# Twelve gate projections beside the long convolution, and the attention share of the mix in the stage behind it

## The chip, the core and the metric

The kernel runs on one core of a Trainium2 chip. The core has five engines that each work through their own queue strictly in order: PE (matrix multiplies), DVE (vector operations), ACT (activation functions and copies), POOL (elementwise, slower) and SP, which starts the DMA transfers here. Semaphores tie the queues together. The metric is the device time of one execution in microseconds (us); the time before is 1934.45 us, the median of three runs (1933.97 to 1934.61).

## What is computed

Two blocks of two layers each work on a sequence of 512 tokens of width 1024, in float32. The change touches the two layers of the first block. Of such a layer the reference says:

```python
q, k, v, z_a, u_h, z_h, g_a, g_h = jnp.split(rms_norm(x) @ w_in, ...)
o = diff_attention(q, k, v, ...)                       # 4 heads
y_a = rms_norm(o) * jax.nn.silu(z_a)                   # 512 x 512
hv, hx1, hx2 = jnp.split(short_conv3(u_h, ...), 3, axis=-1)
z = fft_long_conv(hv, filt[:, 0], ...) * hx1           # order 0
z = fft_long_conv(z, filt[:, 1], ...) * hx2            # order 1
y_h = z * jax.nn.silu(z_h)                             # 512 x 512
m = jax.nn.sigmoid(g_a) * (y_a @ w_pa) + jax.nn.sigmoid(g_h) * (y_h @ w_ph)
x = x + rms_norm(m @ w_out)
```

`g_a` and `g_h` are the gates: each is 1024 channels, eight groups of 128. They need only the normed input, so they may be computed at any time in the layer. `y_a @ w_pa` needs the attention; `y_h @ w_ph` needs the end of the convolution.

## The kernel before

Activations stand as 128 channels by 512 tokens. Each matrix product is made of three passes over a high and a low half of both operands (`mm3`, lines 261 to 263). A **projection** (`projT` over the 1024 input channels) is 24 matmuls of 512 columns into one bank of PSUM; a **branch** (`projT` over 512 channels) is 12. Either takes its weights from `wchunk`: a 512 KB transfer into one of two buffers `wr`, then ACT makes the high half `wh` (line 269) and DVE the low half `wl` (line 270), which for every third chunk is POOL's. PSUM banks for projections come in turn from two `acc` and one `fl`.

`gate` is one projection and a tanh on ACT. `branch` is 12 matmuls; its result is read by a DVE instruction that multiplies it with the gate plus one (line 854 for the attention's share, line 901 for the convolution's).

`hyena` is the long convolution. It runs over two orders `o` and two halves `g` of the channels, four **rounds** in all. One round is a chain through the engines:

- DVE makes sums and differences `sds`, `qd` of two channel groups (lines 751 to 755); PE transposes them (761); ACT and DVE split the result into `sd`.
- For `j` = 0, 1: PE multiplies with the transform into two `lg` banks, 12 matmuls of 256 columns (`px`, `py`); ACT copies one to `ys`; DVE rotates into `w` (784 to 788), multiplies with the filter's spectrum `hs` (791, 792); POOL adds (793, 794); DVE rotates into `Y[j]` (798 to 802).
- For each of the two channel groups: one projection with its short convolution into `hx` (in order 1 a second one, `gz`), the inverse transform as eight matmuls into the one `av` bank (820), which need `Y[0]` and `Y[1]`; DVE takes `e` out of the bank (822), makes `y` (824 to 828), and POOL multiplies `y` with `hx` into the next `z` (829).

Order 1 of a half starts from order 0's `z`. After every `j` step `hyena` calls `next(br)`, which runs one step of `branch_a`: one attention branch for f = 0 to 3, and a gate plus a branch for f = 4 to 7 (the gates 0 to 3 were made beside the attention). After `hyena` the mix stage splits `z` into `yh` and does, for eight `f`, a gate projection, a branch of `yh`, and the chain DVE (901), POOL (902), ACT (272), DVE (273) that leaves the output `m` in two halves. `out1` behind it multiplies with `w_out`.

The kernel is written in this order, but the order of each engine's queue is set at build time by a scheduler, which simulates the program with its own costs. It can pull independent projections forward and put them where it believes PE would wait.

Of the kernel before, what the change touches and what calls it, by code (L numbers as in the profile page):

```python
# [11 lines left out]
F32R = mybir.dt.float32r  # L12
# [4 lines left out]
ADD, SUB, MUL, MAX = ALU.add, ALU.subtract, ALU.mult, ALU.max  # L17

P = 128
S = 512  # L20
# [151 lines left out]
class Kern:  # L172
# [554 lines left out]

    def hyena(self, l, h, br):

        nc, A = self.nc, self.A  # L730
        fbh = self.sm(8, "fbh")
        nc.vector.tensor_scalar(fbh, self.c1[:, C1_FB:C1_FB + 8], 0.25, None, op0=MUL)
        z = self.z
# [3 lines left out]
        iv = self.T("iv", (P, 2, 2, P))  # L737
        nc.sync.dma_start(iv, A["inv"])
        stt = nc.vector.scalar_tensor_tensor
        halves = lambda t: t.rearrange("p (m two) -> p two m", two=2)  # L740
        for o in range(2):
            zn = self.U() if o == 0 else z
            for g in range(2):
                qd = []
                sd_hi = self.T("sd", (P, 2, 2, 256), F32R)
                sd_lo = self.T("sd", (P, 2, 2, 256), F32R)
                for c in range(2):
                    u = z[:, 2 * g + c]
                    up, down = halves(u[:, 0:256]), halves(u[:, 511:255:-1])
                    sd = self.T("sds", (P, 4, P))  # L750
# [14 lines left out]
                for j in range(2):  # L765
# [34 lines left out]
                    else:  # L800
                        stt(x, w[0], cot, w[1], op0=MUL, op1=ADD)
                        stt(y, w[1], cot, w[0], op0=MUL, op1=SUB)
                    next(br, None)
                for c in range(2):
# [23 lines left out]
                    nc.vector.tensor_tensor(halves(y[:, 511:255:-1]), ee[:, 0:2], ee[:, 2:4], op=SUB)  # L828
                    nc.gpsimd.tensor_tensor(zn[:, ct], y, hx, op=MUL)
            z = zn  # L830
        return z
# [12 lines left out]

    def branch_a(self, l, h, ya, ma):

        ma.append(self.U())
        for f in range(8):
            if f % 2 == 0:
                wch = self.wchunk(self.A[f"wpa{l}"][f // 2], 4, 256)  # L850
            t = ma[f // 4][:, f % 4]
            if f > 3:
                self.gate(l, h, 32 + f, t)
            self.nc.vector.scalar_tensor_tensor(t, t, 1.0, self.branch(ya, f, wch), op0=ADD, op1=MUL)
            yield

    def layer1(self, l, h):
# [20 lines left out]
        if "ya" in self.dbg:  # L878
            self.dump(ya, "ya")
        with self.stage(f"h{l}", dict(Y=4, iv=1, hx=2, gz=1, e=2, y=1)), \  # L880
                self.stage(f"i{l}", dict(sd=2, sds=2, qd=4, hs=4, w=4, ab=2)):
            br = self.branch_a(l, h, ya, ma)
            z = self.hyena(l, h, br)
            for _ in br:
                pass
        with self.stage(f"g{l}", dict(mm=4)):
            mh = [self.T("mm", (P, 4, S), F32R) for _ in range(2)]
            ml = [self.T("mm", (P, 4, S), F32R) for _ in range(2)]
            with self.stage(f"y{l}", dict(yh=2, m=3)):
                yh, yl = self.T("yh", (P, 4, S), F32R), self.T("yh", (P, 4, S), F32R)  # L890
                for c in range(4):
                    self.split(z[:, c], yh[:, c], yl[:, c], scale=0.5)
                yhp = [(yh[:, k], yl[:, k]) for k in range(4)]
                if "yh" in self.dbg:
                    self.dump(yhp, "yh")
                for f in range(8):
                    if f % 2 == 0:
                        wch = self.wchunk(A[f"wph{l}"][f // 2], 4, 256)
                    m = self.T("m")
                    self.gate(l, h, 40 + f, m)  # L900
                    nc.vector.scalar_tensor_tensor(m, m, 1.0, self.branch(yhp, f, wch), op0=ADD, op1=MUL)  # L901
                    nc.gpsimd.tensor_tensor(m, m, ma[f // 4][:, f % 4], op=ADD)  # L902
                    self.split(m, mh[f // 4][:, f % 4], ml[f // 4][:, f % 4], scale=0.5)
            m = [(mh[k // 4][:, k % 4], ml[k // 4][:, k % 4]) for k in range(8)]
            with self.stage(f"o{l}", dict(post=1, y1=2, sq2=1, gain=1, sq=1, xn=2)):
                self.out1(l, m)
# [709 lines left out]
```

## Time and profile before

| | us |
|---|---|
| median of three runs | 1934.45 |
| the profiled execution, its own time | 1933.28 |
| span of the profiled execution, first to last instruction | 1931.5 |
| long convolution of layer 0, with the end of the attention | about 200 to 370 |
| mix stage of layer 0 | about 370 to 440 |
| long convolution of layer 1, with the end of the attention | about 690 to 843 |
| mix stage of layer 1 | about 843 to 920 |

PE counts as busy for 97% of the span. A matmul of 512 columns is shown with some 0.39 us, but the next one starts 0.225 us later: they are pipelined, so the busy share hides small losses. What the engine loses shows as idle time between matmuls, and as stretches in which its granted clock is below 1.00.

### The profile page before, as it was taken

The numbers are of one execution on the slowest core, as the hardware profiler recorded it, in microseconds if no ns is written. First come the engines' busy times: TensorE is split into PE (matmuls) and PEld (weight loads), VectorE is DVE, ScalarE is ACT, GpSimd is POOL, SyncE is SP. The second block draws the span as 40 slices with busy tenths as digits, with TensorE's granted clock in tenths as the row PEclk, the third lists the DMA queues.
The fourth block names the chain that finished last, engine by engine and source line by source line (L and its number), as shares of the span: only waits on it lengthen the run. The fifth ranks groups of instructions, "written<-read, shape, count | busy, mean of one in ns | idle before, by whom it ended". The sixth has DMA issues, their size and how long they took to land.

```text
span 1931.5 us, 26186 instructions
## 1 busy us (share of the span) xinstructions
PE 1882.2 (97%) x9632; PEld 1565.8 (81%) x9632; DVE 1294.6 (67%) x2278; ACT 890.4 (46%) x1732; POOL 653.9 (34%) x555
## 2 busy tenths in 40 slices
PE   8999989999999899999999999999999999999998
PEld 5878878888788777888888877888889887788886
DVE  5888698634698868864558856667244886666722
ACT  4666412334476532233456355556324635556631
POOL 2445344432245524533135424211113532421111
PEclk9999989999999999999999999999999999999999
DMA  5333423224323333323432231212343223111232
GB/s 180 105 115 97 158 88 97 100 98 164 113 96 115 101 127 99 109 98 120 133 111 77 82 90 39 64 49 82 131 143 101 77 77 96 39 64 47 84 131 87
DMA packets 88392, 192.35 MB, mean 100 GB/s; under 512 B 28258, under 2 KB 38498, under 8 KB 88264
## 3 DMA queue, kind: packets, MB, share of 16 engines
q1 hardware_dynamic: 69592, 184.84, 29.2%
q10 hardware_dynamic: 17376, 3.67, 1.0%
q0 software_dynamic: 1296, 2.16, 0.4%
q8 instruction: 76, 1.25, 0.3%
q14 instruction: 52, 0.43, 0.1%
HBM read 172.28 MB, written 18.37 MB: 99 GB/s over the span
## 4 chain that ended last, share of the span: by engine, by line
PE 52%; DVE 6%; ACT 1%; issue 1%; POOL 1%; DMA 1%; ACTq 1%; POOLq 0%; DVEq 0%
PE acc L263 8%; PE acc L262 8%; PE acc L261 8%; PE fl L261 4%; PE fl L262 4%; PE fl L263 4%; PE av L1166 2%; DVE u L1373 2%; DVE s L1371 1%; PE av L262 1%; PE av L261 1%; PE av L263 1%; PE lg L1470 1%; PE lg L1462 1%; DVE wl L270 1%
## 5 line engine op out<-in xcount | busy, mean ns | idle before, releaser
L269 ACT ACTIVATE wh<-wr 128x1024 fp32r<-128x1024 f32 (+3 forms) x268 | 256.1, 956 | 393.8 <-PE acc L262 161.8
L262 PE MATMUL acc<-u,wh 128*128 128x512 f32 x1000 | 397.8, 398 | 0.0
L261 PE MATMUL acc<-u,wh 128*128 128x512 f32 x1000 | 397.1, 397 | 0.2
L263 PE MATMUL acc<-u,wl 128*128 128x512 f32 x1000 | 395.2, 395 | 0.0
L270 POOL TENSOR_TENSOR wl<-wr,wh 128x1024 fp32r<-128x1024 f32 (+3 forms) x86 | 186.4, 2168 | 510.9 <-ACT wh L269 422.1
L270 DVE TENSOR_TENSOR wl<-wr,wh 128x1024 fp32r<-128x1024 f32 (+3 forms) x182 | 210.4, 1156 | 165.9 <-ACT wh L269 164.9
L261 PEld LDWEIGHTS acc<-u,wh 128*128 128x128 f32 x1000 | 189.2, 189 | 42.8 <-issue 3.4
L263 PEld LDWEIGHTS acc<-u,wl 128*128 128x128 f32 x1000 | 188.9, 189 | 42.5 <-issue 4.9
L262 PEld LDWEIGHTS acc<-u,wh 128*128 128x128 f32 x1000 | 189.2, 189 | 39.3 <-issue 2.5
L261 PE MATMUL fl<-u,wh 128*128 128x512 f32 x312 | 125.5, 402 | 2.2 <-ACT u L837 2.2
L263 PE MATMUL fl<-u,wl 128*128 128x512 f32 x312 | 123.7, 396 | 0.0
L262 PE MATMUL fl<-u,wh 128*128 128x512 f32 x312 | 123.3, 395 | 0.0
L263 PE MATMUL acc<-wh,u 128*128 128x512 f32 (+1 forms) x212 | 79.3, 374 | 0.3
L262 PE MATMUL acc<-wl,u 128*128 128x512 f32 (+1 forms) x212 | 79.4, 374 | 0.0
L261 PE MATMUL acc<-wh,u 128*128 128x512 f32 (+1 forms) x212 | 77.8, 375 | 0.4 <-ACT u L269 0.2
L261 PEld LDWEIGHTS fl<-u,wh 128*128 128x128 f32 x312 | 59.1, 190 | 15.2 <-ACT u L837 2.4
L263 PEld LDWEIGHTS fl<-u,wl 128*128 128x128 f32 x312 | 59.2, 190 | 12.3
L262 PEld LDWEIGHTS fl<-u,wh 128*128 128x128 f32 x312 | 59.3, 190 | 12.0 <-issue 0.8
L679 ACT ACTIVATE p<-p,mx 128x512 f32<-128x512 f32 x64 | 45.6, 714 | 48.6 <-DVE mx L677 48.6
L324 ACT ACTIVATE sq<-x 128x512 f32<-128x512 f32 x40 | 25.3, 631 | 61.5 <-DVE x L1569 38.7
L793 POOL TENSOR_TENSOR w<-w,ab 128x256 f32<-128x256 f32 x32 | 32.1, 1005 | 54.9 <-DVE w L792 48.4
L902 POOL TENSOR_TENSOR m<-m,u 128x512 f32<-128x512 f32 x16 | 24.7, 1545 | 66.3 <-DVE m L901 66.3
(610 smaller groups left out, 4495.6 us busy)
## 6 DMA issues: line engine op xcount, KB each, us to landing
wr<-in_win SPq DMA_DIRECT2D x88, 512.0 KB, 3.4
wr<-in_xin SPq DMA_DIRECT2D x64, 512.0 KB, 3.4
wr<-in_xout SPq DMA_DIRECT2D x32, 512.0 KB, 3.5
hd<-f SPq DMA_DIRECT2D x32, 256.0 KB, 2.9
hs<-hd SPq DMA_DIRECT2D x32, 256.0 KB, 3.6
wr<-in_wout SPq DMA_DIRECT2D x16, 512.0 KB, 3.5
xd<-x SPq DMA_DIRECT2D x12, 512.0 KB, 2.9
x<-xd SPq DMA_DIRECT2D x12, 512.0 KB, 3.9
```

Of the source, the lines that this page charges most:

```text
L261: mm(ps, l[0], r[0], start=first, stop=False)
L262: mm(ps, l[0], r[1], start=False, stop=False)
L263: return mm(ps, l[1], r[0], start=False, stop=last)
L269: nc.scalar.activation(hi, src, AF.Copy)
L270: (nc.gpsimd if pool else nc.vector).tensor_tensor(lo, src, hi.bitcast(F32), op=SUB)
L324: self.nc.scalar.activation(self.T("sq"), self.xt(i)[:, h * S:(h + 1) * S], AF.Square, scale=1.0 / math.sqrt(D), accum_out=self.ms2[i][:, ...
L679: nc.scalar.activation(pp[c], pp[c], AF.Exp, bias=mx[:, c:c + 1], accum_out=s0[:, i:i + 1] if c == 0 else s)
L793: nc.gpsimd.tensor_tensor(a[:, 0], a[:, 0], b[:, 1], op=ADD)
L902: nc.gpsimd.tensor_tensor(m, m, ma[f // 4][:, f % 4], op=ADD)
L1166: mm(po[:, ts], v[hd // 4][:, k, (hd % 4) * P:(hd % 4 + 1) * P], w[:, k], start=k == 0, stop=k == i)
L1371: nc.vector.tensor_tensor(t, a[:, j, c:].unsqueeze(2).to_broadcast([64, r, c]), m[:, j:j + 1, :c].to_broadcast([64, r, c]), op=MUL)
L1373: nc.vector.tensor_tensor(m[:, c:, :c], m[:, c:, :c], t, op=SUB)
```

## The change

`branch_a` is gone. A generator `gates` makes the last four attention gates and all eight convolution gates, twelve projections, and `hyena` takes two of them after every `j` step of order 0 and one after every `j` step of order 1. The eight attention branches (`part_a`) go into the mix stage: four ahead of the split of `z`, four between the first four convolution branches (`part_h`). The convolution gates wait in `mg` (one U buffer and a new tile); to make room `sds` has one buffer instead of two, and `z` is written in place.

```diff
-    def hyena(self, l, h, br):
+    def hyena(self, l, h, gates):
...
-            zn = self.U() if o == 0 else z
...
-                    next(br, None)
+                    for _ in range(2 - o):
+                        next(gates)
...
-                    nc.gpsimd.tensor_tensor(zn[:, ct], y, hx, op=MUL)
-            z = zn
+                    nc.gpsimd.tensor_tensor(z[:, ct], y, hx, op=MUL)
...
-    def branch_a(self, l, h, ya, ma):
+    def gates(self, l, h, ma, mg):
         ma.append(self.U())
+        mg += [self.U(), self.T("mg", (P, 4, S))]
+        for f in range(4, 8):
+            self.gate(l, h, 32 + f, ma[1][:, f - 4])
+            yield
         for f in range(8):
-            if f % 2 == 0:
-                wch = self.wchunk(self.A[f"wpa{l}"][f // 2], 4, 256)
-            t = ma[f // 4][:, f % 4]
-            if f > 3:
-                self.gate(l, h, 32 + f, t)
-            self.nc.vector.scalar_tensor_tensor(t, t, 1.0, self.branch(ya, f, wch), op0=ADD, op1=MUL)
+            self.gate(l, h, 40 + f, mg[f // 4][:, f % 4])
             yield
...
-                self.stage(f"i{l}", dict(sd=2, sds=2, qd=4, hs=4, w=4, ab=2)):
-            br = self.branch_a(l, h, ya, ma)
-            z = self.hyena(l, h, br)
...
+                    self.stage(f"i{l}", dict(sd=2, sds=1, qd=4, hs=4, w=4, ab=2)):
+                z = self.hyena(l, h, self.gates(l, h, ma, mg))
+            self.mix1(l, h, ya, z, ma, mg)
...
+                def part_a(f):
+                    if f % 2 == 0:
+                        part_a.w = self.wchunk(A[f"wpa{l}"][f // 2], 4, 256)
+                    t = ma[f // 4][:, f % 4]
+                    stt(t, t, 1.0, self.branch(ya, f, part_a.w), op0=ADD, op1=MUL)
+
+                def part_h(f):
+                    if f % 2 == 0:
+                        part_h.w = self.wchunk(A[f"wph{l}"][f // 2], 4, 256)
+                    m = self.T("m")
+                    stt(m, mg[f // 4][:, f % 4], 1.0, self.branch(yhp, f, part_h.w), op0=ADD, op1=MUL)
+                    nc.gpsimd.tensor_tensor(m, m, ma[f // 4][:, f % 4], op=ADD)
+                    self.split(m, mh[f // 4][:, f % 4], ml[f // 4][:, f % 4], scale=0.5)
+
+                for f in range(4):
+                    part_a(f)
+                ends()
...
                 for f in range(8):
-                    if f % 2 == 0:
-                        wch = self.wchunk(A[f"wph{l}"][f // 2], 4, 256)
-                    m = self.T("m")
-                    self.gate(l, h, 40 + f, m)
-                    nc.vector.scalar_tensor_tensor(m, m, 1.0, self.branch(yhp, f, wch), op0=ADD, op1=MUL)
...
+                    part_h(f)
+                    if f < 4:
+                        part_a(4 + f)
```

No instruction of work is added or taken away: both programs have 8730 matmuls. The scheduler's order on PE is the same in both ahead of layer 0's convolution, through most of layer 1's attention, and from layer 1's `out1` to the end.

First place, PE in layer 1, the end of the attention. `av_1234` is the last head's values, `tr_1335` the transposes of the attention's output `o`, which DVE normalizes first, and `tr_1355` the first round's transposes. Before:

```order
L761 MATMUL ft_1406_6594<-ident_66,qd_1403_6585 128x128 x2
L761 MATMUL ft_1406_6594<-ident_66,qd_1405_6591 128x128 x2
L590 MATMUL av_1234_5828<-v_905_4399,wt_1330_6230 128x128 x4
L641 MATMUL tr_1335_6248<-ident_66,o_1333_6239 128x128 x4
L761 MATMUL tr_1355_6358<-ident_66,qd_1351_6342 128x128 x2
L761 MATMUL tr_1355_6358<-ident_66,qd_1353_6348 128x128 x2
L261 MATMUL acc_1370_6409<-u_926_4538,wh_1368_6404 128x512
```

After (the same transposes are `tr_1336`; `acc_1391` is a gate, `acc_1395` a projection of `hx`):

```order
L261 MATMUL acc_1391_6545<-u_844_4097,wh_1393_6547 128x512
L262 MATMUL acc_1391_6545<-u_846_4099,wh_1393_6547 128x512
L263 MATMUL acc_1391_6545<-u_844_4097,wl_1394_6548 128x512
L261 MATMUL acc_1395_6577<-u_843_4096,wh_1397_6579 128x512
L262 MATMUL acc_1395_6577<-u_845_4098,wh_1397_6579 128x512
L263 MATMUL acc_1395_6577<-u_843_4096,wl_1398_6580 128x512
L641 MATMUL tr_1336_6253<-ident_66,o_1334_6244 128x128 x4
```

Before, nothing stood between the last `av` and the transposes that need its result; now 34 matmuls of 512 columns do (7 of one gate, 24 of the next, 3 of `hx`).

Second place, PE in layer 0, the end of order 0's first half. `av_591` (before) and `av_614` (after) are the first inverse transform of the second half; the bank they write is the one that `av_549` (after: `av_561`) filled and that DVE's `e` must have emptied. Before:

```order
L261 MATMUL acc_629_2825<-u_79_438,wh_623_2788 128x512
L262 MATMUL acc_629_2825<-u_80_439,wh_623_2788 128x512
L263 MATMUL acc_629_2825<-u_79_438,wl_624_2789 128x512
L820 MATMUL av_591_2651<-iv_499_2234,Y_570_2542 128x128
L761 MATMUL ft_610_2736<-ident_66,qd_607_2727 128x128 x2
L761 MATMUL tr_611_2743<-ident_66,qd_607_2727 128x128 x2
```

After:

```order
L261 MATMUL fl_609_2808<-u_5_95,wh_611_2810 128x512
L262 MATMUL fl_609_2808<-u_7_97,wh_611_2810 128x512
L263 MATMUL fl_609_2808<-u_5_95,wl_612_2811 128x512
L820 MATMUL av_614_2843<-iv_499_2237,Y_582_2640 128x128
L820 MATMUL av_614_2843<-iv_499_2237,Y_600_2741 128x128
```

Between the two inverse transforms stood 12 matmuls of one attention branch (`acc_629`); now there are 54, of two gates and one `hx` projection (6, 24 and 24).

Third place, DVE at the same point. Before:

```order
L792 TENSOR_TENSOR w_580_2584<-w_580_2584,hs_575_2565 128x512
L792 TENSOR_TENSOR w_581_2585<-w_581_2585,hs_576_2567 128x512
L270 TENSOR_TENSOR wl_648_2925<-wr_646_2923,wh_647_2924 128x1024
L751 TENSOR_TENSOR sds_606_2724<-u_500_2236 128x256
L752 TENSOR_TENSOR sds_606_2724<-u_500_2236 128x256
L822 SCALAR_TENSOR_TENSOR e_550_2471<-qd_506_2248,fbh_497_2229,av_549_2462 128x512
```

After:

```order
L791 TENSOR_TENSOR w_596_2726<-w_596_2726,hs_591_2707 128x512
L750 TENSOR_TENSOR sds_629_2916<-u_183_871 128x256
L751 TENSOR_TENSOR sds_629_2916<-u_183_871 128x256
L791 TENSOR_TENSOR w_597_2727<-w_597_2727,hs_592_2709 128x512
L822 SCALAR_TENSOR_TENSOR e_562_2569<-qd_505_2250,fbh_497_2232,av_561_2560 128x512
```

In both, the next order's `sds`, which waits for POOL's `z`, stands ahead of the `e` that empties the `av` bank; only the weight split `wl_648` between them has gone elsewhere.

## Rows read from the trace of the kernel before

**Rows 1.** The page's first part: engine, busy us, share of the span, instructions

```profile
PE 1882.2 (97%) x9632; PEld 1565.8 (81%) x9632; DVE 1294.6 (67%) x2278; ACT 890.4 (46%) x1732; POOL 653.9 (34%) x555
```

**Rows 2.** Stretches, layer 0: us; busy of PE, PEld, DVE, ACT, POOL; clock, DMA

```profile
220.00:240.00 20.00, 17.82 (x97) 14.62 (x96) 11.02 (x17) 6.66 (x16) 4.16 (x5) 1.00 0.24 80
240.00:260.00 20.00, 18.75 (x95) 15.82 (x94) 18.37 (x22) 4.84 (x8) 9.60 (x9) 1.00 0.32 106
260.00:280.00 20.00, 14.89 (x82) 12.25 (x80) 17.48 (x26) 3.93 (x5) 11.11 (x8) 0.90 0.37 118
280.00:300.00 20.00, 19.70 (x95) 17.16 (x96) 15.47 (x31) 4.66 (x6) 6.35 (x4) 0.85 0.10 29
...
380.00:400.00 20.00, 20.00 (x89) 16.36 (x88) 6.35 (x8) 6.20 (x9) 7.16 (x4) 1.00 0.27 89
```

**Rows 3.** The same view of layer 1

```profile
700.00:720.00 20.00, 15.80 (x79) 13.20 (x78) 12.05 (x18) 6.27 (x16) 7.99 (x7) 0.83 0.29 93
...
740.00:760.00 20.00, 16.64 (x71) 13.45 (x70) 19.50 (x34) 3.95 (x6) 7.73 (x6) 0.83 0.30 104
```

**Rows 4.** PE in order of time, layer 0: start, us, what [idle before, releaser]

```profile
227.36 0.63 PE L641 MATMUL tr<-ident,o 128*128 128x128 f32 x4 [1.10 <-DVE o L638]
...
268.30 1.95 PE L820 MATMUL av<-iv,Y 128*128 128x128 f32 x16
...
272.59 0.39 PE L263 MATMUL acc<-u,wl 128*128 128x512 f32 x1
277.64 0.80 PE L820 MATMUL av<-iv,Y 128*128 128x128 f32 x2 [4.66 <-DVE e L822]
...
283.89 0.63 PE L262 MATMUL acc<-u,wh 128*128 128x512 f32 x1
284.31 0.63 PE L263 MATMUL acc<-u,wl 128*128 128x512 f32 x1
```

**Rows 5.** The same view of layer 1

```profile
703.76 1.08 PE L641 MATMUL tr<-ident,o 128*128 128x128 f32 x4 [3.35 <-DVE o L638]
705.69 1.11 PE L761 MATMUL tr<-ident,qd 128*128 128x128 f32 x4 [0.84 <-DVE o L642]
...
748.27 0.49 PE L820 MATMUL av<-iv,Y 128*128 128x128 f32 x2 [1.14 <-DVE e L822]
750.99 0.80 PE L261 MATMUL fl<-u,wh 128*128 128x512 f32 x1 [2.22 <-ACT u L837]
```

**Rows 6.** POOL and DVE in order of time at layer 0's longest wait

```profile
271.72 3.38 POOL L829 TENSOR_TENSOR u<-y,hx 128x512 f32<-128x512 f32 x1 [5.81 <-DVE y L828]
...
275.14 0.93 DVE L751 TENSOR_TENSOR sds<-u 128x256 f32<-128x256 f32 x1 [1.16 <-POOL u L829]
...
276.85 0.73 DVE L822 SCALAR_TENSOR_TENSOR e<-qd,fbh,av 128x512 f32<-128x512 f32 x1
```

**Rows 7.** DVE alone over order 0 of layer 0 and of layer 1: stretch, busy (instructions)

```profile
229.40:292.40 63.00, 54.09 (x78) 0.92 0.32 104
705.70:768.40 62.70, 53.86 (x81) 0.92 0.29 93
```

**Rows 8.** DVE's weight splits grouped (us, mean ns); one POOL split and its neighbour

```profile
L270 DVE TENSOR_TENSOR wl<-wr,wh 128x1024 fp32r<-128x1024 f32 x16 | 20.3, 1268 | 5.9 <-ACT wh L269 5.9
...
241.28 2.40 POOL L270 TENSOR_TENSOR wl<-wr,wh 128x1024 fp32r<-128x1024 f32 x1
...
241.57 2.67 DVE L798 SCALAR_TENSOR_TENSOR Y<-w,rot,w 128x512 f32<-128x512 f32 x1
```

**Rows 9.** The mix stage's chain, grouped: ns min/median/max, first and last start

```profile
L902 POOL TENSOR_TENSOR m<-m,u x16: 1280/1294/2350, 383.9 to 910.4; 128x512 f32<-128x512 f32 x16
L272 ACT ACTIVATE mm<-m x16: 631/632/634, 385.2 to 911.7; 128x512 fp32r<-128x512 f32 x16
L273 DVE SCALAR_TENSOR_TENSOR mm<-m,mm x16: 679/693/2207, 386.2 to 912.3; 128x512 fp32r<-128x512 f32 x16
...
L901 DVE SCALAR_TENSOR_TENSOR m<-m,acc x11: 673/686/690, 386.8 to 909.5; 128x512 f32<-128x512 f32 x11
```

More of the change, by code (lines that the diff above doesn't have):

```diff
@@ L879, in layer1, with mix1 @@
             self.dump(ya, "ya")
-        with self.stage(f"h{l}", dict(Y=4, iv=1, hx=2, gz=1, e=2, y=1)), \
-                self.stage(f"i{l}", dict(sd=2, sds=2, qd=4, hs=4, w=4, ab=2)):
-            br = self.branch_a(l, h, ya, ma)
-            z = self.hyena(l, h, br)
-            for _ in br:
-                pass
+        with self.stage(f"b{l}", dict(mg=1)):
+            mg = []
+            with self.stage(f"h{l}", dict(Y=4, iv=1, hx=2, gz=1, e=2, y=1)), \
+                    self.stage(f"i{l}", dict(sd=2, sds=1, qd=4, hs=4, w=4, ab=2)):
+                z = self.hyena(l, h, self.gates(l, h, ma, mg))
+            self.mix1(l, h, ya, z, ma, mg)
+    def mix1(self, l, h, ya, z, ma, mg):
+        nc, A = self.nc, self.A
+        stt = nc.vector.scalar_tensor_tensor
         with self.stage(f"g{l}", dict(mm=4)):
@@ L889, in layer1, with ends @@
             with self.stage(f"y{l}", dict(yh=2, m=3)):
[L890 to L893, printed above, removed]
+                yhp = []
+                def ends():
+                    yh, yl = self.T("yh", (P, 4, S), F32R), self.T("yh", (P, 4, S), F32R)
+                    for c in range(4):
+                        self.split(z[:, c], yh[:, c], yl[:, c], scale=0.5)
+                        yhp.append((yh[:, c], yl[:, c]))
+                def part_a(f):
[13 more added lines that the diff above has]
+                ends()
                 if "yh" in self.dbg:
@@ L896, in layer1 @@
                 for f in range(8):
-                    if f % 2 == 0:
-                        wch = self.wchunk(A[f"wph{l}"][f // 2], 4, 256)
-                    m = self.T("m")
-                    self.gate(l, h, 40 + f, m)
-                    nc.vector.scalar_tensor_tensor(m, m, 1.0, self.branch(yhp, f, wch), op0=ADD, op1=MUL)
-                    nc.gpsimd.tensor_tensor(m, m, ma[f // 4][:, f % 4], op=ADD)
-                    self.split(m, mh[f // 4][:, f % 4], ml[f // 4][:, f % 4], scale=0.5)
+                    part_h(f)
+                    if f < 4:
+                        part_a(4 + f)
             m = [(mh[k // 4][:, k % 4], ml[k // 4][:, k % 4]) for k in range(8)]
```

## The prediction

> **What bounds the kernel now.** The first thing to read is the page's engine line: PE is busy 97% of the span, DVE 67%, the others less [rows 1]. PE is the bound on average, so only what PE itself loses can be won back, and no term of a sum may be larger than PE's loss in the stage that the change touches. That loss is read from the table of stretches. In the mix stage PE is busy 20.00 of 20 us with 89 matmuls, a pitch of 20 / 89 = 0.225 us for 512 columns, at a clock of 1.00 [rows 2]: nothing is lost there. In order 0 of the convolution and at the end of the attention it does lose. Layer 0: 2.18 + 1.25 + 5.11 + 0.30 = 8.8 us idle between 220 and 300 us [rows 2]. Layer 1: 4.20 + 3.36 = 7.6 us in its two bad stretches [rows 3]. Together 16.4 us.
>
> The shown idle time is a little short, since a matmul counts as busy for 0.39 us and the next follows after 0.225: from 272.59 to 277.64 PE lost 5.05 - 0.23 = 4.8 us, with 4.66 shown [rows 4]. Some ten waits at 0.17 each add 1.7 us.
>
> Then the clock. It fell to 1.2 GHz after the long waits: the stretches show 0.90 and 0.85 [rows 2], 0.83 and 0.83 [rows 3]. At half speed that is 4.0 + 6.0 + 6.8 + 6.8 = 23.6 us of time, and 512 columns took 0.42 us there (283.89 to 284.31 [rows 4]) instead of 0.225. If PE worked in all of it, it lost half, 11.8 us. If all the idle time of those four stretches (5.1 + 0.3 + 4.2 + 3.4 = 13.0 us) lay within it, (23.6 - 13.0) / 2 = 5.3 us. I take the middle, 8.5.
>
> So PE loses 16.4 + 1.7 + 8.5 = 26.6 us in the two convolutions (21.7 to 29.9 by the bounds). What ends each wait last is in the timelines: the attention's output `o` (DVE, line 638) before its transposes, and `e` (DVE, line 822) before the `av` bank is free [rows 4, 5]. DVE was not slow there, it was late: `e` stands behind `sds`, and `sds` waited for POOL's product with `z`, which took 3.38 us [rows 6].
>
> **The change part by part.** *Nothing is added.* Matmuls, tanhs, weight splits and transfers are the same in number; all is a move, so each edit costs zero unless an engine waits differently.
>
> *The gates in the convolution.* A gate is 24 matmuls, 5.4 us of PE, against 2.7 us of a branch, and it needs only the normed input. What matters is how many matmuls stand at the places where PE waited.
>
> End of the attention: PE was ready 3.35 us (layer 1) and 1.10 us (layer 0) before `o` [rows 4, 5]. Now 34 matmuls, 7.7 us, stand between the last values and these transposes, in both layers. The need is under 4 us, so the wait goes, and so does the one behind it (0.84 us [rows 5]), because the first round's transposes now come some 20 matmuls after those of `o`. What is late next is the first round itself, which starts later by PE's own work; that costs nothing while PE is full.
>
> The `av` bank, layer 0: 12 matmuls (2.7 us) plus a wait of 4.8 us made 7.5 us between the two inverse transforms. Now 54 matmuls, 12.2 us, stand there: covered, with 4.7 us to spare. Layer 1: 7 matmuls plus 1.14 us of wait, some 3 us, were needed [rows 5]; now 27 matmuls, 6.1 us. Covered too, but if POOL there takes as long as in layer 0 (7.5 us needed) 1.4 us stay. The third wait, 2.22 us for a bank that ACT's tanh had to empty [rows 5], came from a branch pulled into a bank just filled; in the new order two projections lie between a bank's users.
>
> Is DVE fast enough once PE no longer waits? From the first round's second transposes to the last inverse transform of order 0, the new order has in layer 0 197 matmuls of 512 columns (44.3 us) and 127 narrow records of about 0.12 us (the `av` row gives 1.95 / 16 [rows 4]), 15.3 us: 59.6 us of PE. In layer 1 it is 181 and 132: 56.6 us. DVE was busy 54.1 and 53.9 us over the same work [rows 7]. It loses five reads of attention branches at 0.69 (the same kind of instruction as line 901 [rows 9]) and gains one weight split at 1.27 [rows 8]: 54.1 - 3.4 + 1.3 = 52.0 and 51.7 us. So DVE has 7.6 and 4.9 us of room. Its chain also has waits for ACT and POOL of its own, so I leave 1 us in all as what PE still waits, between 0 and the first rival below.
>
> *The mix stage.* It loses 65 - 43 = 22 us of PE work (a gate of 24 for each of eight `f`), which is the same work that the convolution gained. Its cover at the start is equal: two gates, 48 matmuls, stood ahead of the first use of `yh`, now four attention branches, 48 matmuls, 10.8 us. The chain behind a convolution branch is 0.69 + 1.29 + 0.63 + 0.69 = 3.3 us [rows 9], and the last four branches now follow each other every 2.7 us. Only its first link empties a PSUM bank, and there are three banks, so I take 0; the bound is 4 x (3.3 - 2.7) = 2.4 us a layer, 4.8 us in all.
>
> *The smaller edits.* One `sds` buffer instead of two: writer and reader are both DVE, which works in order, so nothing waits; 0. `z` in place: its readers of the same half have run in the same queue chain; 0. SP's queue: the gates' chunks stand among the `hs` loads, one 512 KB chunk for 5.4 us of PE, the rate at which the mix stage already runs without loss [rows 2]; 0.
>
> Sum: 1933.3 - 26.6 + 1.0 = 1907.7 us against the profiled execution's own time. The median of the runs is 1.2 us above that execution, so the forecast is **1908.9 us**.
>
> A rule of the skill speaks against the move. The row: a DVE rotation took 2.67 us while a POOL weight split of 2.40 us ran beside it [rows 8], where one of its kind takes 0.73 alone [rows 6]. The Trainium skill (SBUF — State Buffer, section "Who interferes with whom") says that a DVE instruction with two SBUF inputs and a GpSimd instruction that reads SBUF share a port pair by an exclusive lock, and whichever comes second waits; the trace agrees. By that rule every third chunk brought into the convolution would cost DVE 1.9 us: four more chunks in order 0 are 1.3 splits, 2.6 us a layer. The new order, though, has two POOL splits among order 0's rounds of layer 0, as many as before, so the sum stays.
>
> **The rivals.** *DVE's rounds are as long as they were.* Order 0 took 63.0 and 62.7 us [rows 7]. If these were DVE's and POOL's own chain and not PE's waits, PE still waits 63.0 - 59.6 = 3.4 and 62.7 - 56.6 = 6.1 us, and the clock falls behind such waits as it did, say for half of its cost, 4.3 us. Then 13.8 us stay: 1933.3 - 26.6 + 13.8 + 1.2 = 1921.7 us. For it: DVE was busy 86% of these stretches. Against: its idle time, 8.9 us in each, contains waits for what PE had not yet done.
>
> *The gain is lost again to the chunks.* Eight gates are now wanted in order 0, each needing a transfer, ACT and DVE or POOL in queues that are full of the rounds. If each of the 16 waited 1.7 us for its `wl`, the 26.6 us are back: about 1934 us. For it: splits stand in DVE's queue among rotations. Against: in the new order each stands far ahead of its use.
>
> *Slower.* The gates ahead of the chain's matmuls in PE's queue make each round late, and the single `av` bank with `e` behind `sds` stalls in every round, not in one per layer: a stall costs 4.8 us plus some 3.5 us of low clock. It decides from the fourth of eight rounds; five would be 41.5 - 26.6 = 15 us, 1949 us. Against: the counts of 54 and 27 matmuls at exactly these places.
>
> **How the numbers follow.** Forecast (1904 to 1914): 0.63. DVE as slow as before (1914 to 1927): 0.22. Chunks, no net gain: 0.08. Slower: 0.07. A difference below 0.2%, 3.9 us, can't be told from none here. So faster 0.85, same 0.08, slower 0.07. The range for 8 in 10 begins at 1903.5 (26.6 replaced by the upper bound of 29.9, and what remains at 0: 1904.6, with 1 us for the runs) and goes up into the second case, to 1924.
>
> **What would show it.** Right: in the profile after, PE's clock reads 1.00 through both convolutions, the waits for `o` and `e` are gone, and PE's idle time from 220 to 300 us is under 2 us. The rival: waits at `av` for lines 801 and 802 (the `Y` rotation) with DVE over 95% busy in order 0. The chunks: PE waiting for line 270. Wrong altogether: idle time on PE in the mix stage, or waits for `e` in most rounds.

## The result, and the profile after

| | before | after |
|---|---|---|
| median of four runs each, us | 1934.21 (1932.79 to 1934.61) | 1915.99 (1915.07 to 1916.37) |
| span of the profiled execution, us | 1931.5 | 1914.6 |

The ratio is 0.9905, with an interval of 0.9892 to 0.9917: 18.2 us faster, where 25.5 were forecast (1908.9). The time lies within the range of 1903.5 to 1924.

The engine line of the page after answers to [rows 1]; its columns are engine, busy us, share of the span and instructions.

```profile
PE 1870.7 (98%) x9632; PEld 1557.9 (81%) x9632; DVE 1286.2 (67%) x2278; ACT 889.1 (46%) x1732; POOL 649.5 (34%) x555
```

The instruction counts are the same as before. The next two views are the stretches of the kernel after, with the columns of [rows 2]: us; busy of PE, PEld, DVE, ACT, POOL; clock, DMA. First layer 0, which answers to [rows 2]:

```profile
220.00:240.00 20.00, 20.00 (x98) 16.68 (x97) 5.01 (x8) 8.10 (x18) 4.67 (x3) 1.00 0.28 91
...
260.00:280.00 20.00, 20.00 (x116) 17.49 (x115) 17.96 (x27) 4.94 (x8) 9.12 (x9) 1.00 0.32 100
280.00:300.00 20.00, 20.00 (x110) 17.17 (x108) 17.10 (x25) 6.09 (x8) 9.29 (x7) 1.00 0.33 106
300.00:320.00 20.00, 18.48 (x92) 15.19 (x91) 16.40 (x29) 5.58 (x8) 6.29 (x6) 1.00 0.32 105
```

Then layer 1, which answers to [rows 3]:

```profile
700.00:720.00 20.00, 20.00 (x108) 17.05 (x107) 10.25 (x14) 6.89 (x10) 5.43 (x4) 1.00 0.32 104
...
740.00:760.00 20.00, 18.64 (x99) 15.44 (x98) 19.23 (x28) 5.12 (x6) 11.46 (x8) 1.00 0.29 96
...
780.00:800.00 20.00, 17.38 (x78) 14.45 (x77) 16.72 (x22) 5.00 (x6) 10.51 (x9) 0.91 0.31 106
```

From 220 to 300 us PE is full and at 2.4 GHz (clock 1.00), where it had lost 8.8 us and run at 0.90 and 0.85. In layer 1 it is full at 700 to 720 us. But behind that there are other waits, of which the kernel before had none or less (its 3.36 us at 740 to 760 were for `e` and for a bank that ACT empties [rows 5]): 1.5 us at 300 to 320, 1.4 at 740 to 760, 2.6 with the clock at 0.91 at 780 to 800. A fourth is in `out1` of layer 0, behind the mix.

What PE waits for there shows in its order of time (start, us, what, and in brackets the idle time before it and its releaser). The transposes of `o` start without a bracket, where [rows 4, 5] had 1.10 and 3.35 us, and so do the inverse transforms of order 0 in layer 0, where they had 4.66:

```profile
231.47 0.60 PE L641 MATMUL tr<-ident,o 128*128 128x128 f32 x4
...
287.22 1.95 PE L820 MATMUL av<-iv,Y 128*128 128x128 f32 x16
...
304.69 0.39 PE L262 MATMUL lg<-sd,x 128*128 128x256 f32 x1 [1.34 <-DVE sd L270]
...
447.20 0.50 PE L261 MATMUL fl<-u,mm 128*128 128x512 f32 x1 [1.64 <-DVE u L959]
...
700.22 0.60 PE L641 MATMUL tr<-ident,o 128*128 128x128 f32 x4
...
756.57 1.16 PE L820 MATMUL av<-iv,Y 128*128 128x128 f32 x8 [0.67 <-DVE Y L800]
...
791.58 2.67 PE L820 MATMUL av<-iv,Y 128*128 128x128 f32 x13 [2.62 <-DVE Y L800]
```

So the old waits are gone and new, smaller ones stand elsewhere: in order 1's first round of either layer (304.69 and 791.58), at the end of order 0 in layer 1 (756.57), and in `out1` (447.20).

The wait at 791.58 is the longest. DVE and POOL in order of time ahead of it:

```profile
773.88 3.42 POOL L829 TENSOR_TENSOR u<-y,hx 128x512 f32<-128x512 f32 x1 [6.31 <-DVE y L828]
...
780.41 2.58 POOL L270 TENSOR_TENSOR wl<-wr,wh 128x1024 fp32r<-128x1024 f32 x1
...
790.02 0.72 POOL L793 TENSOR_TENSOR w<-w,ab 128x256 f32<-128x256 f32 x1
...
773.66 1.28 DVE L790 TENSOR_TENSOR ab<-w,hs 128x512 f32<-128x512 f32 x2
774.86 1.28 DVE L791 TENSOR_TENSOR w<-w,hs 128x512 f32<-128x512 f32 x2
777.33 0.95 DVE L750 TENSOR_TENSOR sds<-u 128x256 f32<-128x256 f32 x1 [1.19 <-POOL u L829]
...
780.65 2.62 DVE L754 TENSOR_TENSOR qd<-sds 128x256 f32<-128x256 f32 x1
...
790.78 0.75 DVE L800 SCALAR_TENSOR_TENSOR Y<-w,rot,w 128x512 f32<-128x512 f32 x1 [0.65 <-POOL w L793]
```

POOL's product into `z` took 3.42 us beside four products of DVE, and DVE waited 1.19 for it; then POOL split a weight chunk for 2.58 us, and the DVE operation beside it took 2.62 where the same instruction takes 0.42 at 301.65 (754 is the line of `qd`). That the last sums of POOL and the rotation `Y` come late by this, 7 us later, is an inference here; a run below tries it. The wait at 304.69 has the same sign: a POOL split and a DVE `sds` beside it.

```profile
298.25 2.41 POOL L270 TENSOR_TENSOR wl<-wr,wh 128x1024 fp32r<-128x1024 f32 x1
...
298.33 2.60 DVE L750 TENSOR_TENSOR sds<-u 128x256 f32<-128x256 f32 x1 [1.47 <-POOL u L829]
```

In `out1` PE waits for a bank that DVE line 959 must read, and that stands in DVE's queue behind a weight split that waits for ACT, and ACT for a transfer. Here are SP, ACT and DVE after, and then SP, DVE and PE of the kernel before at the same place:

```profile
435.04 6.12 SPq L283 DMA_DIRECT2D wr<-in_wout  x3
...
444.23 1.06 ACT L269 ACTIVATE u<-wr 128x1024 fp32r<-128x1024 f32 x1 [2.19 <-DMA wr<-in_wout]
...
445.32 1.23 DVE L270 TENSOR_TENSOR u<-wr,u 128x1024 fp32r<-128x1024 f32 x1 [4.51 <-ACT u L269]
446.46 0.68 DVE L959 TENSOR_TENSOR u<-fl,post 128x512 f32<-128x512 f32 x1
```

```profile
444.10 6.11 SPq L283 DMA_DIRECT2D wr<-in_wout  x3
...
455.50 0.68 DVE L938 TENSOR_TENSOR u<-fl,post 128x512 f32<-128x512 f32 x1
...
458.10 0.40 PE L261 MATMUL fl<-u,mm 128*128 128x512 f32 x1
```

From the issue of the second three transfers to DVE's read it is 11.4 us in both (435.04 to 446.46, 444.10 to 455.50). Before, PE wanted the bank 14.0 us after the issue; now it was ready for it after 10.5 (447.20 - 1.64 - 435.04). So the transfers start too late, by the work of the mix stage ahead of them and not by `out1`'s; a run below tries that.

### The profile page after: what moved, and what is told of

The parts are those of the page before. It is cut to its first block, busy times and chain, and to the rows that moved or that the text cites. A ratio compares the mean times of both kernels' runs of the same rounds, so it can differ in the third digit from the quotient of the medians.

```text
span 1914.6 us, 26170 instructions
## 1 busy us (share of the span) xinstructions
PE 1870.7 (98%) x9632; PEld 1557.9 (81%) x9632; DVE 1286.2 (67%) x2278; ACT 889.1 (46%) x1732; POOL 649.5 (34%) x555
## 4 chain that ended last, share of the span: by engine, by line
PE 76%; DVE 12%; issue 3%; POOL 3%; ACT 3%; DMA 3%; ACTq 1%; SPq 0%; DVEq 0%; POOLq 0%
PE acc L263 13%; PE acc L261 13%; PE acc L262 13%; PE fl L261 5%; PE fl L262 5%; PE fl L263 5%; PE av L1187 2%; DVE u L1394 1%; DVE s L1392 1%; PE av L820 1%; PE av L261 1%; PE av L262 1%; PE av L263 1%; DVE wl L270 1%; PE av L590 1%
## 5 line engine op out<-in xcount | busy, mean ns | idle before, releaser
L1174 ACT ACTIVATE p<-p,amx 128x128 f32<-128x128 f32 (+1 forms) x64 | 35.7, 558 | 23.3 <-DVE amx L1173 23.2
```

The lines of the kernel that those rows point to most:

```text
L1174: nc.scalar.activation(p[:, :n], p[:, :n], AF.Exp, bias=mx, scale=scale, accum_out=s)
```

## The experiments

The theory is the prediction's: the gain is PE's **cover**, the independent matmuls that stand ahead of a place where it would wait, and what is left over are the two new losses, in the convolutions and in `out1`. The rivals are the small edits, the relief of DVE by the branches that left, and POOL's weight splits as the one cause. Runs of the kernel before stood beside all of them (medians 1932.9 to 1933.8).

| | us | ratio to before, 95% |
|---|---|---|
| after | 1916.0 | 0.9905 (0.9892 to 0.9917) |
| e1 small edits alone | 1932.8 | 0.9995 (0.9986 to 1.0005) |
| e4 gates dealt 1 and 2 | 1929.2 | 0.9976 (0.9966 to 0.9985) |
| e3 gates and four branches | 1907.9 | 0.9870 (0.9855 to 0.9885) |
| e6 after, no POOL splits in the convolution | 1907.6 | 0.9864 (0.9848 to 0.9881) |
| e9 before, no POOL splits in the convolution | 1933.1 | 0.9998 (0.9989 to 1.0008) |
| e10, e10b POOL splits one or two chunks later | 1914.4, 1914.8 | 0.9905 and 0.9906 (0.9888 to 0.9921) |
| e5 last branches apart | 1914.1 | 0.9898 (0.9883 to 0.9912) |
| e7 is e5 and e6 | 1906.3 | 0.9859 (0.9845 to 0.9874) |
| e8 is e7, no POOL splits in the layer | 1908.3 | 0.9872 (0.9855 to 0.9888) |
| e12 is e7, none in layer 1's attention either | 1898.8 | 0.9822 (0.9807 to 0.9837) |
| e11 is e3, none in both convolutions and layer 1's attention | 1897.8 | 0.9818 (0.9803 to 0.9832) |

**The small edits alone.** To the kernel before:

```diff
-            zn = self.U() if o == 0 else z
...
-                    nc.gpsimd.tensor_tensor(zn[:, ct], y, hx, op=MUL)
-            z = zn
+                    nc.gpsimd.tensor_tensor(z[:, ct], y, hx, op=MUL)
...
-                self.stage(f"i{l}", dict(sd=2, sds=2, qd=4, hs=4, w=4, ab=2)):
+                self.stage(f"i{l}", dict(sd=2, sds=1, qd=4, hs=4, w=4, ab=2)):
```

> The kernel before with the two small edits alone: sds with one buffer, z written in place; the attention branches stay beside the convolution and the gates in the mix. Theory (the gain is the gates that now stand where PE waited): the places before the transposes of o and between the inverse transforms are as empty as before (0 and 12 matmuls in layer 0), so the time is that of the kernel before, within 2 us, 1932 to 1936. Rival (the one buffer and the in-place z free the chain of the rounds): at least 5 us of the 18 us of gain appear, 1929 or less.

It measured 1932.8, a ratio of 0.9995. The bad stretch of layer 0 is that of the kernel before within 0.3 us ([rows 2] has 14.89):

```profile
260.00:280.00 20.00, 14.65 (x81) 12.05 (x79) 17.50 (x27) 3.67 (x5) 11.12 (x8) 0.89 0.36 118
```

No time is seen for the small edits; the theory stands.

**The gates dealt the other way.** To the kernel after:

```diff
-                    for _ in range(2 - o):
+                    for _ in range(1 + o):
```

> The changed kernel with the twelve gates dealt the other way round: one after every step of order 0, two after every step of order 1. The attention branches stay in the mix, so DVE is relieved of their reads as in the changed kernel. By the order on PE 34 and 31 matmuls still stand ahead of the transposes of o, but only 12 (layer 0) and none (layer 1) between the two inverse transforms where e must empty the av bank. Theory (cover on PE): the waits for o stay away, the waits at av in order 0 come back with 3 to 5 us in each layer and a half clock behind them, and the late wait of layer 1's order 1 shrinks: 1922 to 1930 us. Rival (relief of DVE by the branches that left): 1914 to 1918 us, with no wait at av over 1 us in order 0.

It measured 1929.2, as the theory has it: three quarters of the gain are gone, though DVE is as free of the branches' reads as in the kernel after. PE in order of time shows where:

```profile
278.73 0.49 PE L820 MATMUL av<-iv,Y 128*128 128x128 f32 x2 [2.72 <-DVE e L822]
...
328.32 1.16 PE L820 MATMUL av<-iv,Y 128*128 128x128 f32 x8 [1.57 <-DVE Y L800]
...
757.40 0.68 PE L820 MATMUL av<-iv,Y 128*128 128x128 f32 x2 [4.09 <-DVE e L822]
```

The waits for `e` are back with 12 and 0 matmuls ahead of them, and 700 to 720 us, where 31 matmuls stand ahead of `o`, is free (20.00 busy at 1.00). Cover is what counts at these places. The late wait of layer 1's order 1 is gone, but one thing was not as expected: order 1 of layer 0, with two gates a step, waits too (328.32).

**Gates and four branches.** `gates` also runs an attention branch after every second gate of order 0, so the mix has four fewer (the loop over `n`, the twelve gates, is cut):

```diff
...
+            if n % 2 and n < 8:
+                f = n // 2
+                if f % 2 == 0:
+                    wch = self.wchunk(self.A[f"wpa{l}"][f // 2], 4, 256)
+                t = ma[0][:, f]
+                self.nc.vector.scalar_tensor_tensor(t, t, 1.0, self.branch(ya, f, wch), op0=ADD, op1=MUL)
             yield
...
-                for f in range(4):
+                for f in range(4, 8):
                     part_a(f)
...
                     part_h(f)
-                    if f < 4:
-                        part_a(4 + f)
```

> The changed kernel with four of the eight attention branches taken back beside the convolution, one after every step of order 0, so that both gates and these branches stand there; the other four stand ahead of the split of z in the mix, and the last eight convolution branches follow each other. Theory (cover on PE is what counts, not DVE's relief by the branches that left): order 0 stays free of waits over 2 us, since PE has 48 more matmuls there against four DVE reads of 0.69 us; the waits in out1 stay or grow by 1 to 3 us, since all convolution branches are now back to back: 1914 to 1920 us. Rival (the reads of the branches on DVE were what made order 0 wait): waits at av or o in order 0 return, 1922 us or more.

It measured 1907.9, under the 1914 to 1920 us expected, and 7 to 8 us better than the kernel after (6.8 by the ratios, 8.1 by the medians). With four of the branches' reads back on DVE order 0 has no wait, so DVE's relief by them is no part of the gain that shows. PE's waits in both convolutions (those of 0.15 us and more) sum to 2.3 us, against 5.7 in the kernel after, the clock is 1.00 throughout, and this is the longest in layer 0:

```profile
336.56 0.94 PE L820 MATMUL av<-iv,Y 128*128 128x128 f32 x6 [0.98 <-DVE Y L801]
```

That it is the 12 matmuls of each branch that help there is likely, but was not tried apart from the other mix. The expectation for `out1` was a miss: all eight branches of `yh` follow each other here, and PE doesn't wait in `out1` at all.

**No POOL splits in the convolution.** `wchunk` gives its POOL splits to DVE while `self.busy` is set:

```diff
+                self.busy = True
                 z = self.hyena(l, h, self.gates(l, h, ma, mg))
+                self.busy = False
```

> The changed kernel with POOL's share of the weight splits inside the convolution given to DVE. Theory (what PE still waits in layer 1's convolution comes from POOL: its split of 2.6 us stretches a DVE operation beside it and makes its own product and sums late): the loss of clock and the waits at av between 740 and 800 us fall, some 3 to 5 us of gain, 1911 to 1913 us. Rival (DVE has too much work there): about five more splits of 1.27 us in each layer make the waits longer, 1918 us or more.

It measured 1907.6, so 8.4 us of what was left are gone (7.9 by the ratios), more than the 3 to 5 us expected. PE's waits in both convolutions sum to 0.7 us. The three bad stretches of the kernel after, here:

```profile
300.00:320.00 20.00, 20.00 (x101) 16.94 (x100) 17.13 (x28) 5.90 (x8) 8.12 (x8) 1.00 0.32 102
...
740.00:760.00 20.00, 19.57 (x106) 16.52 (x106) 19.97 (x31) 4.68 (x7) 7.88 (x6) 1.00 0.32 104
...
780.00:800.00 20.00, 19.75 (x107) 16.78 (x106) 18.16 (x27) 5.90 (x8) 8.06 (x7) 1.00 0.43 144
```

DVE has more to do, not less. Its groups in layer 1's convolution (690 to 840 us), of the kernel after and then of this one; the columns are line, engine, operation, out<-in, count, busy us, mean ns, idle before:

```profile
L270 DVE TENSOR_TENSOR wl<-wr,wh 128x1024 fp32r<-128x1024 f32 x14 | 17.6, 1256 | 13.0 <-ACT wh L269 13.0
...
L754 DVE TENSOR_TENSOR qd<-sds 128x256 f32<-128x256 f32 x4 | 6.1, 1517 | 0.0
...
L797 DVE SCALAR_TENSOR_TENSOR Y<-w,rot,w 128x512 f32<-128x512 f32 x4 | 4.9, 1216 | 0.2 <-POOL w L793 0.2
```

```profile
L270 DVE TENSOR_TENSOR wl<-wr,wh 128x1024 fp32r<-128x1024 f32 x21 | 27.8, 1324 | 16.6 <-ACT wh L269 16.6
...
L797 DVE SCALAR_TENSOR_TENSOR Y<-w,rot,w 128x512 f32<-128x512 f32 x4 | 3.0, 743 | 0.0
...
L754 DVE TENSOR_TENSOR qd<-sds 128x256 f32<-128x256 f32 x4 | 2.7, 687 | 0.0
```

Seven more splits cost DVE 10.2 us, and lines 754 and 797 got 5.3 us back. The sum is against DVE, and still PE waits less. POOL's long product is still there (3.41 us, at 769.40), so it was the splits. A split on POOL holds up the DVE operation that happens to stand beside it, as at 298.33 and 780.65 above. That the scheduler places the splits on DVE where the chain can bear them, and doesn't know of what POOL's do, is inferred from the places, not shown.

**The same edit to the kernel before.**

```diff
+            self.busy = True
             br = self.branch_a(l, h, ya, ma)
             z = self.hyena(l, h, br)
             for _ in br:
                 pass
+            self.busy = False
```

> The kernel before with no POOL weight splits inside the convolution, all else as it was. The places on PE ahead of the transposes of o and between the inverse transforms stay as empty as they were (0 matmuls, and 12 and 13). Theory (PE's loss before is a want of cover; POOL's splits add to it only in the waits for e behind POOL's product of 3.38 us): 2 to 7 us of gain, 1927 to 1932 us, and the waits for o stay. Rival (POOL's splits alone are the cause, and the gates only happened to move them): most of the 18 us, 1920 us or less.

It measured 1933.1: nothing, less than either theory gave. PE still waits for `o`, and in layer 0, where it hardly waits for `e`, it waits for the next thing of DVE, the read of a branch:

```profile
275.53 0.80 PE L261 MATMUL acc<-u,wh 128*128 128x512 f32 x1 [4.30 <-DVE u L854]
...
698.30 1.09 PE L641 MATMUL tr<-ident,o 128*128 128x128 f32 x4 [3.35 <-DVE o L638]
```

In layer 1 it waits 3.55 us for DVE's `qd` at 749.26. So POOL's splits are not the cause of the old loss. The same edit is worth nothing without the gates and 8.4 us with them.

**POOL's splits at other chunks.** Is it POOL's splits, or the bad place of two of them? To the kernel after, with 1 and then with 2, the count of chunks that picks the third is shifted inside the convolution:

```diff
+                self.wn += 1
                 z = self.hyena(l, h, self.gates(l, h, ma, mg))
+                self.wn -= 1
```

> The changed kernel with POOL still taking every third weight split inside the convolution, but the chunk after the one that it takes now. As many POOL splits as before, at other places. Theory A (POOL's splits as such cost the chain): the convolutions lose about as much as in the changed kernel, 1914 to 1918 us. Theory B (it was the place of one or two of them, at 303 and 780 us, that cost): the time falls most of the way to that without POOL splits, 1907 to 1911 us.

> The same with the second chunk after. Theory A (POOL's splits as such): 1914 to 1918 us in this one too. Theory B (the place): the three phases scatter over 3 us or more, and the time of each follows from whether a POOL split stands beside the chain of DVE that PE waits for at the end of a round.

They measured 1914.4 and 1914.8, about the ratio of the kernel after (0.9905). PE's waits in both convolutions sum to 7.0 and 5.7 us, where the kernel after has 5.7. Some stand elsewhere, at 325.61 in the first, at 328.65 and 763.89 in the second; layer 1's wait for `Y` stays in the first, with 1.88 us at 790.41:

```profile
325.61 1.83 PE L820 MATMUL av<-iv,Y 128*128 128x128 f32 x14 [1.81 <-DVE Y L800]
```

```profile
328.65 1.83 PE L820 MATMUL av<-iv,Y 128*128 128x128 f32 x14 [2.68 <-DVE Y L800]
...
763.89 0.44 PE L760 MATMUL ft<-ident,qd 128*128 128x128 f32 x2 [1.95 <-DVE qd L753]
```

So it is POOL's splits as such and not the place of two of them. Is it also that PE's cover is short? It can be counted: the matmuls of 512 columns that stand on PE between the last inverse transform of order 0 and the first of order 1 that needs `Y[1]`. Beside it stand PE's waits for `Y[1]` there, and what it had waited shortly ahead, in the second half of order 0 or for `sd`.

| kernel, layer | matmuls | POOL splits | wait for `Y[1]`, us | waits ahead, us |
|---|---|---|---|---|
| after, 1 | 83 | yes | 2.62 | 0.67, 0.52, 0.21 |
| e10, 1 | 94 | yes | 1.88 | 0.68, 0.52, 0.72 |
| e4, 0 | 96 | yes | 1.57, 1.59 | 2.72, 2.77 |
| e10b, 1 | 96 | yes | 0 | 1.95 |
| before, 1 | 99 | yes | 0 | 1.14, 2.22 |
| e4, 1 | 102 | yes | 0 | 4.09, 0.91, 1.27 |
| before, 0 | 106 | yes | 0.34 | 4.66, 0.56 |
| e10, 0 | 106 | yes | 1.81 | 1.35 |
| e10b, 0 | 106 | yes | 2.68 | 0.57, 0.51 |
| e3, 0 | 106 | yes | 0.98 | 0 |
| after, 0 | 116 | yes | 0 | 1.34, 0.18 |
| e3, 1 | 116 | yes | 0 | 1.12, 0.18 |
| e6, 1 | 93 | no | 0.26 | 0.43 |
| e6, 0; e11, 0 and 1 | 106 | no | 0 | 0 |

With the gates and without POOL splits, 93 matmuls are nearly enough and 106 are enough. With POOL splits every row has waits, there or shortly ahead, and the count doesn't tell how long: with 106 it is 0.34 to 2.68 us, and the two rows with 116 had lost 1.3 to 1.5 us for `sd` just ahead. The kernel before has little or no wait at `Y[1]` with 99 and 106; its stalls in order 0 may have let DVE come up, but e4 waits in layer 0 behind such stalls too. How much cover would hide the splits is not shown.

**The last branches apart.** To the kernel after:

```diff
                 for f in range(8):
+                    if f > 3:
+                        part_a(f)
                     part_h(f)
-                    if f < 4:
-                        part_a(4 + f)
```

> The changed kernel with the mix in another order: the last four attention branches stand one ahead of each of the last four convolution branches, so that those no longer follow each other every 2.7 us. Theory (the chains of the last convolution branches hold up ACT's and DVE's splits of out1's weights, so the transfers of the second half start late): the two waits in out1 behind DVE line 959, 1.6 to 2.5 us each, fall to under 0.5 us, and the time falls by 3 to 4.5 us to 1911.5 to 1913 us. Rival (out1 waits for its weights because the gates no longer spread the transfers): the waits stay and so does the time, 1915 to 1917 us.

The wait behind line 959 is gone. SP and DVE at that place:

```profile
431.40 6.13 SPq L283 DMA_DIRECT2D wr<-in_wout  x3
...
442.81 0.68 DVE L959 TENSOR_TENSOR u<-fl,post 128x512 f32<-128x512 f32 x1
```

The transfers start 3.6 us earlier (1.0 us of it because this kernel is that much ahead from the transposes of `o` on). The time fell by 1.9 us, by the medians, not by 3 to 4.5, and the two intervals overlap, so it is the trace and not the time that shows it. The expectation counted a wait in layer 1's `out1` that is none: from 900 to 940 us PE is full in the kernel after. And the cause is not that branches follow each other as such, since the kernel with eight in a row (e3) doesn't wait either; what is left as the cause is how late the last of them and the weight splits behind it run.

**Both.** The two diffs above together.

> The changed kernel with both edits of the runs before: no POOL weight splits inside the convolution, and the last four attention branches one ahead of each of the last four convolution branches. Theory (the two residuals lie in different stages and don't touch each other): the gains add, 1916.0 - 8.4 - 1.9 = 1905.7, so 1904.5 to 1907 us, with PE's idle time below 1 us in both convolutions and the wait behind line 959 gone. Rival (the shorter convolution only moves the wait into out1 or the mix): 1907.5 us or more.

It measured 1906.3: no wait over 0.5 us is shown in either convolution, none in `out1`. The gains add as expected, so the two residuals lie apart.

**No POOL splits in the layer.** e7 with `self.busy` set from the start of the attention to the end of `out1`, in both layers.

```diff
     def attention1(self, l, h, v, flt, zv):
         nc, A = self.nc, self.A
+        self.busy = True
...
             self.mix1(l, h, ya, z, ma, mg)
+            self.busy = False
```

> The combination before, with POOL's share of the weight splits given to DVE in the attention and in the mix and out1 too, all of the first block's two layers but the part ahead of the attention. Theory (POOL's splits hurt where DVE's chain is what PE waits for): the wait of 4.5 us in layer 1's attention behind DVE line 673 has POOL splits of 2.6 us beside it and shrinks by 1 to 3 us; the mix, where DVE is idle two thirds of the time, doesn't change: 1902 to 1906 us. Rival (in the attention DVE is short of time, and about seven more splits of 1.27 us a layer make its waits longer): 1907 us or more.

It measured 1908.3, no gain, where 1902 to 1906 was expected. The wait in layer 1's attention did shrink (from 4.51 to 2.08 and 1.04 us), but in `out1`, where DVE now splits those weights as well, PE waits again, 2.05 us in layer 0 and 1.15 in layer 1, and it waits 1.46 us for `Y` at 291.55 us. That DVE has no room there is the likely reason; the next run leaves these parts out.

**Without POOL splits in layer 1's attention alone.** e7 with `self.busy` also set there; layer 0's attention, the mix and `out1` keep POOL's splits.

```diff
+                self.busy = l == 1
                 ya = self.attention1(l, h, v, flt, self.hyena_v(l, h, ma))
```

> The changed kernel with the mix order in which the last branches stand apart, and without POOL's splits in both convolutions (1906.3 together) and now also in layer 1's attention alone, not in layer 0's, nor in the mix and out1. Theory (without POOL splits everywhere, the gain of layer 1's attention was eaten by the start of the program and by out1): 1906.3 less 4 to 6, so 1900 to 1902.5 us, and the wait behind DVE line 673 shrinks from 4.5 to about 2.3 us. Rival (that attention's gain is lost behind it): 1905 us or more.

It measured 1898.8, 7.5 us under e7 (7.2 by the ratios), more than expected. What it takes away, in POOL and DVE and then on PE of the kernel after:

```profile
633.68 2.79 POOL L270 TENSOR_TENSOR wl<-wr,wh 128x1024 fp32r<-128x1024 f32 x1
...
632.51 4.51 DVE L557 TENSOR_TENSOR f<-f,f 128x512 f32<-128x512 f32 x2
636.94 0.68 DVE L673 CUSTOM_DVE_ANT_0 p<-lg,bias 128x512 f32<-128x512 f32 x1
...
637.68 0.80 PE L669 MATMUL lg<-qk,qk 128*128 128x512 f32 x1 [4.52 <-DVE mx L673]
```

and PE of this kernel at the same instruction:

```profile
625.66 0.50 PE L669 MATMUL lg<-qk,qk 128*128 128x512 f32 x1 [1.91 <-DVE mx L673]
```

Two products on DVE took 4.51 us beside POOL's operations, and the next maximum stood behind them. PE's waits in this attention fall from 5.9 us in e7 to 2.8 here, and the clock from 620 to 640 us reads 0.91 where e7 has 0.83. The wait stands in the kernel before too (4.49 us at 649.40); it was no part of the change.

**The best.** e3's diff, with that of the convolution and that of layer 1's attention:

> The kernel with gates and four branches beside the convolution (the one that measured 1907.9), without POOL's weight splits in both convolutions and in layer 1's attention. Theory (each of these took a wait of its own away): 1907.9 less the 4 us that its convolutions still lose less the 4 to 6 us by which layer 1's attention got shorter without POOL splits: 1898 to 1901 us. Rival (in the convolution the cover by branches and the want of POOL splits repair the same waits, and the attention's gain is eaten further on): 1905 us or more.

It measured 1897.8, a ratio of 0.9818 (0.9803 to 0.9832), the fastest of all, though not to be told from e12. PE is full at 1.00 from 220 to 360 and from 700 to 840 us:

```profile
780.00:800.00 20.00, 20.00 (x110) 17.27 (x109) 13.79 (x20) 5.88 (x9) 5.72 (x6) 1.00 0.33 103
```

## Why the prediction was right, and where its sum was not

The sign and the range held, and so did the mechanism of the gain; one term of the sum failed. Of the signs, PE's idle time from 220 to 300 us is 0 and the waits for `o` and, in order 0, for `e` are gone; the clock is not 1.00 throughout (0.91 at 780 to 800 us). Term by term:

- **PE's loss of 26.6 us** was about right. With both new losses taken away (e7) the time is 27.5 us under that of the runs of before beside it (1933.8 - 1906.3). That is between the bounds of 21.7 and 29.9, in their upper part (the lower one leaves out the 1.7 us of hidden idle time).
- **The waits for `o` and for the `av` bank behind `e`** went as told, in both layers; e4 brought those for `e` back by taking the matmuls away again, and with them the half clock (0.84 at 280 to 300 us).
- **DVE's room in order 0** was right in its main part: over the same work DVE was busy 50.51 us of 59.50 in layer 0 and 49.69 of 59.77 in layer 1, with 52.0 and 51.7 forecast against [rows 7]. PE's own work was 59.5 us in layer 0, as forecast, and 58.4 in layer 1, where 56.6 was.
- **What PE still waits, 1.0 us**, is the step that failed: it was 8.4 us (1916.0 - 1907.6). The sum asked only whether order 0 was covered, since the kernel before lost next to nothing in order 1 ([rows 2, 3] have no bad stretch of it). But the new waits stand at the end of order 0 and in order 1, and they go with POOL's splits (e6, e10). These were set at no change, since order 0 of layer 0 has two of them as before. In both convolutions together there are 13 before and 16 after (of the program's 98, e9 leaves 85 on POOL and e6 82). The rise of three can hardly be it: the 13 cost nothing before (e9), the 16 cost 8.4 us after. The gates also came to order 0 at order 1's cost: each step there had a gate and a branch, 36 matmuls, and has a gate, 24. In layer 1 the cover ahead of `Y[1]` fell from 99 to 83, and 2.62 us are lost there; in layer 0 it rose from 106 to 116, so the cover can be a part of it in layer 1 alone, and no run gave it back by itself.
- **The mix stage, 0** was right of the mix, where PE is full, but its end cost a wait of 1.64 us in `out1`, about 1.9 us of time (e5). The bound of 4.8 us held it. The prediction looked at whether the chain's first link frees its bank, and not at what else stands in ACT's and DVE's queues behind the chain: the splits that let `out1`'s second transfers start.
- **The small edits, 0**: right (e1).
- **The 1.2 us between profile and median**: the new profiled execution stands 0.4 us above its median.

Of the rivals, "DVE's rounds are as long as they were" is what came in part: its sign, waits at `av` for the rotation lines 800 and 801 with DVE busy 19.23 of 20 us, shows at 740 to 760 us of layer 1, with 0.67 and 0.52 us. The longer waits are in order 1, for which it was not told. The transfers of the chunks and the stall in every round did not come.

The row that the prediction weighed against the move says more than was made of it. In the runs, the 128x256 DVE operation at 780.65 took 2.62 us beside POOL's split of 2.58, and POOL's product took 3.42 us beside DVE's products and ended 1.2 us behind the last of them, where another of its kind took 1.28 in all at 766.29. The Trainium skill (SBUF — State Buffer, section "Who interferes with whom") has the rule for both, one lock on a port pair that the two engines share, and the trace agrees. What such a stretch cost the program the runs had to tell: nothing while PE waited for something else anyway (e9), and 8.4 us once that chain of DVE was what PE waited for (e6). The 2.6 us a layer that the prediction worked out for such stretches and set aside was nearer the mark than the 0 that it took.

What stays open: how much cover would hide POOL's splits, why the kernel before hardly waits at `Y[1]` with 99 and 106 matmuls where e10 waits with 94 and 106, and why e8 waits at 291.55 us of layer 0, where e7 doesn't.

## What to carry to other kernels

When independent work is moved to where an engine waits, count the cover at both ends: at the place that gets it, and at the place it came from, with the chain of the other engines that was hidden there. Here the gain at the first is shown; the cost at the second is likely in one layer of two. A helper engine's share that measured as free while something else was the bound has to be measured again once that something is gone; here the same edit was worth 0 us before the change and 8.4 us behind it. And look past the stage that is edited to the first transfer that its chains hold up.

## What the runs showed of the hardware that was not expected

A weight split on POOL (2.4 to 2.8 us) cost more than the same split on DVE (1.2 to 1.3 us), counted in time: in the convolution 8.4 us, in layer 1's attention 7.5 us, without any change of the work; in the kernel before, in the convolution, nothing. Two DVE products of 128x512 of line 557 were shown with 4.51 us beside POOL's operations; the shortest of that line takes 0.67 us and the median one 1.23.

PE's clock fell to half behind the wait of 2.62 us at 791.58 (0.91 in that stretch) and stayed at 1.00 behind those of 1.34 and 1.64 us. But the length of the wait alone does not decide it: behind the 2.68 us at 328.65 in e10b it stayed at 1.00, and in layer 1's attention it fell behind 1.91 us in e12 (0.91 from 620 to 640 us) and not behind 1.99 in e11. The stretch of e10b:

```profile
320.00:340.00 20.00, 17.32 (x90) 14.43 (x89) 15.17 (x18) 4.32 (x6) 9.47 (x7) 1.00 0.32 106
```
